# First products of a transformer layer: the statistics of x moved from VectorE to ScalarE, modulation columns by transposes, the first weights in four parts

## The chip, the cores and the metric

The kernel runs on one core of a Trainium2 chip. The metric is the device time of one execution in microseconds (us). The engines are named as the profile does: PE (TensorE, matrix products), PEld (its weight loads), DVE (VectorE), ACT (ScalarE), POOL (GpSimd) and SP (SyncE, which here issues nearly all DMA transfers). Each engine works through its own queue in order; semaphores hold it back where it needs another engine's result.

## What is computed

One layer on 256 tokens of 2048 features in float32: a gated feed-forward part (5632 hidden features), a token mixer (8 attention heads and 4 recurrent heads), and a second feed-forward part. Before each part the tokens are normalised and modulated by a shift and a scale that come from a condition vector c; after each part comes a layer norm with residual.

```python
def _modulate(x, shift, scale):
    return _layernorm(x) * (1 + scale) + shift

def _swiglu(h, w_in, w_out):
    gate, up = jnp.split(h @ w_in, 2, axis=-1)
    return (jax.nn.silu(gate) * up) @ w_out

    ada = (jax.nn.silu(c) @ w_ada + b_ada)[:, None, :]
    sh1, sc1, g1, sh2, sc2, g2, sh3, sc3, g3 = jnp.split(ada, N_ADA, axis=-1)
    h = _swiglu(_modulate(x, sh1, sc1), ffn1_w_in, ffn1_w_out)
    x = _layernorm(ALPHA * x + 0.5 * (1 + g1) * h, ln1_g, ln1_b)
    ...
```

For this document only the start matters: sh1 and sc1 (each a product of silu(c) with 2048 x 2048 of w_ada), the mean and variance of each token of x, and the first products with ffn1_w_in.

## The kernel before

The 256 tokens are two halves of 128 (a = 0, 1), one token per partition, in the tile res. Every product is made of three (mm3, L391 to L393): each operand is split into hi, a rounded copy made on ACT, and lo, the remainder made on DVE; hi by hi, hi by lo and lo by hi are added up in PSUM. PE does only these products, transposes and small sums.

The first modulation is made in four blocks j of 512 features. For a block, first_ada (L702) fetches 16 rows of w_ada, 512 KB each, one DMA transfer each (L714, L720). Row k holds 128 inputs for 512 columns of the shift and 512 of the scale. DVE adds up raw x silu(c) over the rows into acc (ada_acc, L156 on; L158 for row 0, L160 for the others; for block 0 acc lies in the tile gate). The last row is added in two halves of the columns. What remains is a sum over the 128 partitions, and the result has to stand with features on partitions: column (L754) makes it with two products per group of 128 features, acc as the stationary operand and a column of ones as the moving one (L757), and DVE adds the bias columns (L759) into scsh. In the other blocks columns (L738, L741) does so for four groups at once.

ada_acc ends in tc.keep_in_program_order(ins): the instruction is queued behind the last one that was written for the same engine before it. Other instructions are placed by a scheduler, from its own estimate of when operands are there. Where tc.manual_schedule names an engine, that engine takes its instructions in the order of writing.

Beside this, x is normalised. Eight bn_stats on DVE (L845), four for each half of the tokens, and bn_aggr (L281) give mean and variance; row_std (L280) adds EPS on DVE (L283) and takes the inverse root on POOL (L271); L848 makes -mean x root on DVE. These instructions are written before the sixteen rows. modulate_both (L307) then normalises 512 features on ACT (L311), transposes them on PE (L317), and per group of 128 features applies scale and shift (L322, ACT), makes hi (L325, ACT) and lo (L327, DVE).

The weights of the first part come as tiles of 512 inputs by 512 outputs, 1 MB, by one DMA transfer (load_w, L374), and are split two groups of 128 inputs at a time (1024 columns of free size; L145 on ACT, L146 on DVE). The first tile's weights are split inside the last step of first_ada(0), where ws_halves is advanced between the column groups; this step stands under manual_schedule for DVE and ACT (L854). first_in (L792) makes the 48 products of a tile for two PSUM tiles, and ACT copies them out (L812). There are twelve tiles in each of the four blocks.

The buffers: three of 8 KB per partition named raw, shared by the modulation rows (two rows each) and the raw weights; three named araw, which take every third pair of rows; six each of hi and lo. A transfer into a buffer is issued when the last reader of its former content is done, and SP issues in its order. PSUM has five tiles for products (mm_tile) and three for the rest (aux_tile).

## Time and profile before

| | |
|---|---|
| Time, median of 3 runs | 1940.28 us (1939.87 to 1940.95) |
| The profiled execution's own time | 1938.98 us |
| Its span in the profile | 1937.3 us |
| First product (L391) starts | 38.59 us |
| First row of w_ada added (L158) | 13.79 us |
| Last row added (L160) starts | 33.52 us |
| PE busy from 0 to 25 us | 2.46 us |
| PE busy from 25 to 50 us | 14.91 us |
| PE busy from 50 to 75 us | 25.00 us |

Times inside the profile count from the start of its span. A row of the timeline gives start, length, engine, line, operation, the tile written, the tiles read, their shapes, and in brackets how long the engine stood idle before it and what ended the wait. "x4" means that four such instructions were merged into one row. A row of a group gives busy time and, behind the comma, the mean length of one instruction in ns. "SPq" rows are issues of DMA transfers. The profiled execution was 1.3 us shorter than the median.

### The profile page before, as it was taken

To read this page: it belongs to the slowest core of one execution; us is meant where nothing else is said; L and a number is where in the kernel's file an instruction comes from. 1 tells how busy PE (TensorE), PEld (TensorE's weight loads), DVE (VectorE), ACT (ScalarE), POOL (GpSimd) and SP (SyncE) were. 2 spreads that over 40 slices of the span, in tenths; PEclk is the share of its full clock that TensorE was granted. 3 is DMA by queue.
4 is the path that set the end of the run, shared out by engine and by line. 5 is a ranking of instruction groups with operands and counts; after the bars stand their busy time and mean duration, and the time that the engine had idled before them with its cause. 6 is when DMAs were issued, how large, how long until landed. Compare 5 with 4: busy or idle time off the path is not lost.

```text
span 1937.3 us, 32182 instructions
## 1 busy us (share of the span) xinstructions
PE 1886.1 (97%) x13133; PEld 1730.2 (89%) x13133; DVE 1465.4 (76%) x1771; ACT 931.0 (48%) x1296; POOL 19.4 (1%) x37
## 2 busy tenths in 40 slices
PE   3999999999999999999999999999999999999997
PEld 3999999999988888698999776999999999988886
DVE  7778979777778899688787787867776654555776
ACT  2544354444354554745664644555444444444562
POOL 0000000000000000000000000000000000000000
PEclk9999999999999999999999999999999999999999
DMA  8998969999898898489878784997777655655552
GB/s 323 351 314 308 324 217 309 314 315 334 273 341 302 275 310 270 153 297 317 280 240 280 282 289 157 331 305 272 234 264 260 229 195 192 228 194 193 196 193 90
DMA packets 301963, 510.89 MB, mean 264 GB/s; under 512 B 10834, under 2 KB 158962, under 8 KB 300792
## 3 DMA queue, kind: packets, MB, share of 16 engines
q1 hardware_dynamic: 300952, 505.70, 77.0%
q0 software_dynamic: 864, 3.15, 0.6%
q8 instruction: 103, 1.69, 0.4%
q14 instruction: 44, 0.36, 0.1%
HBM read 506.71 MB, written 2.10 MB: 263 GB/s over the span
## 4 chain that ended last, share of the span: by engine, by line
PE 84%; DVE 8%; DMA 4%; ACT 2%; issue 1%; POOL 0%; DVEq 0%; SPq 0%; ACTq 0%; POOLq 0%
PE gu_f L393 8%; PE gu_f L392 8%; PE gu_f L391 8%; PE o_f L391 8%; PE o_f L393 8%; PE o_f L392 8%; DMA raw_s<-in_ffn_w_in_dram 3%; PE s L393 3%; PE s L391 3%; PE s L392 2%; PE pr_f L393 2%; PE pr_f L392 2%; PE pr_f L391 2%; DVE gate L160 2%; PE fh L392 2%; PE fh L393 2%
## 5 line engine op out<-in xcount | busy, mean ns | idle before, releaser
L160 DVE SCALAR_TENSOR_TENSOR acc<-ar,csil,acc 128x1024 f32<-128x1024 f32 x242 | 307.2, 1270 | 25.4 <-DMA ar<-in_w_ada_dram 24.6
L391 PE MATMUL s<-xhi_f,hi_s 128*128 128x256 f32 x768 | 214.0, 279 | 1.2 <-ACT hi_s L145 1.2
L393 PE MATMUL s<-xhi_f,lo_s 128*128 128x256 f32 x768 | 213.4, 279 | 1.6 <-DVE lo_s L146 1.5
L392 PE MATMUL s<-xlo_f,hi_s 128*128 128x256 f32 x768 | 213.3, 278 | 0.0
L393 PE MATMUL gu_f<-xhi_f,lo_f2i 128*128 128x256 f32 x768 | 212.0, 276 | 0.0
L392 PE MATMUL gu_f<-xlo_f,hi_f2i 128*128 128x256 f32 x768 | 212.0, 276 | 0.0
L391 PE MATMUL gu_f<-xhi_f,hi_f2i 128*128 128x256 f32 x768 | 212.0, 276 | 0.0
L146 DVE TENSOR_TENSOR lo_f2i<-raw_f2i,hi_f2i 128x1024 fp32r<-128x1024 f32 x96 | 117.5, 1225 | 99.0 <-ACT hi_f2i L145 98.9
L391 PE MATMUL gu_f<-xhi_f,hi_f1i 128*128 128x256 f32 x640 | 176.8, 276 | 0.0
L393 PE MATMUL gu_f<-xhi_f,lo_f1i 128*128 128x256 f32 x640 | 176.7, 276 | 0.0
L392 PE MATMUL gu_f<-xlo_f,hi_f1i 128*128 128x256 f32 x640 | 176.7, 276 | 0.0
L145 ACT CAST hi_f2i<-raw_f2i 128x1024 fp32r<-128x1024 f32 x96 | 100.8, 1050 | 137.5 <-PE gu_f L392 125.5
L145 ACT CAST hi_s<-raw_s 128x1024 fp32r<-128x1024 f32 x96 | 97.2, 1049 | 105.8 <-DMA raw_s<-in_ffn_w_in_dram 78.9
L393 PEld LDWEIGHTS s<-xhi_f,lo_s 128*128 128x128 f32 x768 | 145.1, 189 | 2.4 <-DVE lo_s L146 2.4
L391 PEld LDWEIGHTS s<-xhi_f,hi_s 128*128 128x128 f32 x768 | 145.4, 190 | 1.6 <-ACT hi_s L145 1.5
L392 PEld LDWEIGHTS s<-xlo_f,hi_s 128*128 128x128 f32 x768 | 145.6, 190 | 0.0
L392 PEld LDWEIGHTS gu_f<-xlo_f,hi_f2i 128*128 128x128 f32 x768 | 144.2, 188 | 0.1
L391 PEld LDWEIGHTS gu_f<-xhi_f,hi_f2i 128*128 128x128 f32 x768 | 144.2, 188 | 0.1
L393 PEld LDWEIGHTS gu_f<-xhi_f,lo_f2i 128*128 128x128 f32 x768 | 144.2, 188 | 0.0
L146 DVE TENSOR_TENSOR lo_s<-raw_s,hi_s 128x1024 fp32r<-128x1024 f32 x96 | 114.5, 1221 | 36.5 <-ACT hi_s L145 34.2
L145 ACT CAST hi_f1i<-raw_f1i 128x1024 fp32r<-128x1024 f32 x80 | 83.3, 1050 | 116.6 <-PE gu_f L392 66.7
L146 DVE TENSOR_TENSOR lo_f2o<-raw_f2o,hi_f2o 128x1024 fp32r<-128x1024 f32 x86 | 105.3, 1224 | 43.2 <-ACT hi_f2o L145 43.1
(483 smaller groups left out, 5336.6 us busy)
## 6 DMA issues: line engine op xcount, KB each, us to landing
ar<-in_w_ada_dram SPq DMA_DIRECT2D x288, 512.0 KB, 5.9
raw_s<-in_ffn_w_in_dram SPq DMA_DIRECT2D x48, 1024.0 KB, 5.4
raw_f2i<-in_ffn_w_in_dram SPq DMA_DIRECT2D x48, 1024.0 KB, 5.1
raw_f1o<-in_ffn_w_out_dram SPq DMA_DIRECT2D x44, 1024.0 KB, 8.0
raw_f2o<-in_ffn_w_out_dram SPq DMA_DIRECT2D x44, 1024.0 KB, 5.1
raw_f1i<-in_ffn_w_in_dram SPq DMA_DIRECT2D x40, 1024.0 KB, 7.8
raw_mxo<-in_w_out_dram SPq DMA_DIRECT2D x16, 1024.0 KB, 7.9
raw_fh<-in_ffn_w_in_dram SPq DMA_DIRECT2D x16, 1024.0 KB, 7.8
```

Of the source, the lines that this page charges most:

```text
L145: S.copy(hi, src)
L146: V.tensor_tensor(out=lo, in0=src, in1=hi.bitcast(F32), op=ALU.subtract)
L160: ins = V.scalar_tensor_tensor(out=acc, in0=raw, scalar=csil[:, k:k + 1], in1=acc, op0=ALU.mult, op1=ALU.add)
L391: PE.matmul(o, ah, bh, start=start, stop=False)
L392: PE.matmul(o, ah, bl, start=False, stop=False)
L393: return PE.matmul(o, al, bh, start=False, stop=stop)
```

## The change

The statistics of x are made on ScalarE: an Identity pass that adds up, two small multiplications (mean and minus mean), a Square pass with minus the mean as bias that adds up, and a multiplication to the variance, for each half of the tokens. row_std runs without bn_aggr, one half after the other. The output of the two passes goes to a part of hT that is not in use yet.

The columns of block 0 are made by transposes: two per group of 128 features into a PSUM tile of its own (one aux_tile, three mm_tile), a sum along the free dimension on DVE, and the bias added by DVE.

The first weights come by four transfers of 256 KB, and are split one group of 128 inputs at a time; the transfers and the first rounded copy are written ahead of the first group's scale and shift, the others between the groups.

```diff
     def row_std(mv, rs, st, tag):
-        V.bn_aggr(mv, st)
-        yield
+        if st is not None:
+            V.bn_aggr(mv, st)
+            yield
...
-        cps = aux_tile(f"cp{j}"), mm_tile(f"cq{j}") if j == 0 else None
+        cps = [aux_tile(f"cp{j}")]
...
+        cps += [mm_tile(f"cq{q}") for q in range(3)]
+
         def column(q):
-            cp = cps[q % 2][:, q:q + 2]
             for v in range(2):
-                PE.matmul(cp[:, v:v + 1], acc[:, v, q * P:(q + 1) * P], ones[:, 0:1], start=True, stop=True)
-            k = 4 * j + q
-            V.tensor_tensor(out=scsh[:, 0:2, k:k + 1], in0=cp.unsqueeze(2), in1=bcol[:, 0:2, k:k + 1], op=ALU.add)
+                PE.transpose(cps[q][:, v * P:(v + 1) * P], acc[:, v, q * P:(q + 1) * P], ident)
+            cs = scsh[:, 0:2, q:q + 1]
+            V.tensor_reduce(out=cs, in_=cps[q][:, :2 * P].rearrange("p (v n) -> p v n", v=2), axis=AX.X, op=ALU.add)
+            V.tensor_tensor(out=cs, in0=cs, in1=bcol[:, 0:2, q:q + 1], op=ALU.add)
 
         column(0)
-        next(mb)
-        column(1)
-        next(mb)
-        next(mb)
-        column(2)
-        next(ws, None)
-        next(mb)
-        column(3)
-        next(mb)
-        next(ws, None)
-        for _ in mb:
-            pass
+        next(ws)
+        for q in range(4):
+            next(mb)
+            if q < 3:
+                column(q + 1)
+            next(mb)
+            next(ws)
+            next(ws, None)
         yield
...
-    def ws_halves():
-        it = first_w(0, 0)
-        for _ in range(2):
-            ws.extend(next(it) for _ in range(2))
+    def first_ws():
+        raw = wp.tile([P, 4, 512], F32, tag="raw", bufs=3, name="raw_first")
+        for k in range(4):
+            SP.dma_start(raw[:, k, :], W1[k * P:(k + 1) * P, :512])
+        parts = [[wp.tile([P, 2, 512], F32R, tag=t, bufs=6, name=f"{t}_first{h}") for h in range(2)]
+                 for t in ("hi", "lo")]
+        for k in range(4):
+            hi, lo = (p[k // 2][:, k % 2, :] for p in parts)
+            S.copy(hi, raw[:, k, :])
             yield
-
-    fa = first_ada(0, ws_halves())
+            V.tensor_tensor(out=lo, in0=raw[:, k, :], in1=hi.bitcast(F32), op=ALU.subtract)
+            ws.append((k, hi, lo))
+            yield
+
+    fa = first_ada(0, first_ws())
...
-    sts = [stat_tile(f"x{a}") for a in range(2)]
+    sq = hT[:, 0:8, :].rearrange("p f t -> p (f t)")
     for a in range(2):
-        for q in range(4):
-            V.bn_stats(sts[a][:, q, :], res[:, a, q * 512:(q + 1) * 512])
-    together(*[row_std(mvx[a], rs0[a][:, 0:1], sts[a], f"x{a}") for a in range(2)])
+        xs = small(10, "sums", f"sums_x{a}")
+        S.activation(sq, res[:, a, :], AF.Identity, accum_out=xs[:, 0:1])
+        S.mul(mvx[a][:, 0:1], xs[:, 0:1], 1.0 / D)
+        S.mul(xs[:, 1:2], xs[:, 0:1], -1.0 / D)
+        S.activation(sq, res[:, a, :], AF.Square, bias=xs[:, 1:2], accum_out=xs[:, 2:3])
+        S.mul(mvx[a][:, 1:2], xs[:, 2:3], 1.0 / D)
+    for a in range(2):
+        for _ in row_std(mvx[a], rs0[a][:, 0:1], None, f"x{a}"):
+            pass
     for a in range(2):
         V.scalar_tensor_tensor(out=rs0[a][:, 1:2], in0=mvx[a][:, 0:1], scalar=-1.0, in1=rs0[a][:, 0:1],
                                op0=ALU.mult, op1=ALU.mult)
```

## The prediction

> **What bounds the kernel now.** First the page, by engine and by its chain that ended last:
>
> ```profile
> PE 1886.1 (97%) x13133; PEld 1730.2 (89%) x13133; DVE 1465.4 (76%) x1771; ACT 931.0 (48%) x1296; POOL 19.4 (1%) x37
> ...
> PE 84%; DVE 8%; DMA 4%; ACT 2%; issue 1%; POOL 0%; DVEq 0%; SPq 0%; ACTq 0%; POOLq 0%
> ```
>
> PE is busy for 97% of the span, so whatever the change can win or lose lies in the small rest, most of it before the first product. That stretch is read from the chain in order of time (start, length, what):
>
> ```profile
> 6.24 2.47 DVE st_x L845 x4
> ...
> 13.79 0.76 DVE gate L158
> ...
> 33.52 0.76 DVE gate L160
> ...
> 34.41 1.00 PE cp L757 x4
> ...
> 37.60 0.95 ACT hi_s L145
> ...
> 38.59 0.58 PE s L391
> ...
> 44.97 0.21 PE s L393
> ...
> 45.47 0.12 PE s L393
> ```
>
> The reader is to see one thread: x lands, its statistics (DVE and POOL), the sixteen rows of the first modulation block on DVE (13.79 to 34.9), their columns, the normalised x, the first weights, the first product at 38.59. Products then step at 0.21 us, and from 45.1 on at 0.12.
>
> How the rows hang on the statistics is in the timeline:
>
> ```profile
> 10.08 2.46 DVE L845 BATCH_NORM_STATS2 st_x<-res 128x6 f32<-128x512 f32 x4
> 12.58 0.26 DVE L281 BATCH_NORM_AGGREGATE mv_x<-st_x 128x2 f32<-128x24 f32 x1
> 12.88 0.15 DVE L283 TENSOR_SCALAR mv_x<-mv_x 128x1 f32<-128x1 f32 x1
> ...
> 13.70 0.16 DVE L848 SCALAR_TENSOR_TENSOR mr_x<-mv_x,mr_x 128x1 f32<-128x1 f32 x1 [0.67 <-POOL mr_x L271]
> ...
> 14.58 6.57 DVE L160 SCALAR_TENSOR_TENSOR gate<-ar,csil,gate 128x1024 f32<-128x1024 f32 x5
> ```
>
> Row 0 (L158, 13.79) starts 0.09 us after L848 for the second half of x. That is no accident: ada_acc ties each row behind the VectorE instruction written before it, and the last one written before row 0 is that L848. DVE takes its queue in order, so **row 0 waits for the statistics of both halves of x**, whoever computes them. From there the rows run without a gap, one per 1.31 us (five in 6.57).
>
> **The change, part by part.**
>
> *1. Statistics on ScalarE.* Eight bn_stats and two aggregations leave DVE (2.47 us and 0.26 us for each half). L283 and L848 stay on DVE, POOL keeps its pow, and row 0 stays tied behind L848. So the freed DVE time is not used by the rows: DVE now waits for ACT. The new ACT work is not in the trace at its size; its nearest rows:
>
> ```profile
> L819 ACT ACTIVATE hT<-hT 128x512 f32<-128x512 f32 x12 | 7.3, 631 | 2.0 <-DVE hT L814 2.0
> L545 ACT ACTIVATE sq<-res,sums 128x768 f32<-128x768 f32 x8 | 7.5, 939 | 1.0 <-DVE res L541 0.8 <-DVE sums L551 0.2
> L545 ACT ACTIVATE sq<-res,sums 128x512 f32<-128x512 f32 x4 | 2.9, 725 | 25.3 <-DVE sums L544 25.3
> L545 ACT ACTIVATION_READ_ACCUMULATOR sq<-res,sums 128x1 f32 x12 | 2.2, 186 | 0.0
> L1241 ACT ACTIVATE table<-ident 128x1 f32<-128x1 f32 x1 | 0.2, 203 | 0.0
> ```
>
> From 512 to 768 elements ACT takes 939 - 725 = 214 ns more, 0.836 ns an element. An Identity over 2048 without a bias column is 631 + 1536 x 0.836 = 1.92 us; a Square with one is 939 + 1280 x 0.836 = 2.01 us. Each is followed by a read of the accumulator (0.19), and there are three multiplications of one column (0.20 each). End to end that is 1.92 + 2.01 + 0.37 + 0.61 = 4.9 us for half of x. ACT instructions overlap by about 0.1 us at a joint:
>
> ```profile
> 775.32 0.73 ACT L545 ACTIVATE sq<-res,sums 128x512 f32<-128x512 f32 x1 [12.48 <-DVE sums L544]
> 775.95 0.19 ACT L545 ACTIVATION_READ_ACCUMULATOR sq<-res,sums 128x1 f32 x1
> ```
>
> (775.32 + 0.73 is 0.10 past 775.95). With all six joints overlapped it is 4.3 us. Most joints are between an instruction and the reader of its result, so I take 4.6, and keep 4.3 to 4.9. The first half starts when x lands (6.24), the second right behind it, since its data are there by 10.08: done at 6.24 + 9.2 = 15.4. L283 follows at 15.5 against 12.88, and the rest of the thread (POOL, L848, row 0) is unchanged at 0.91 us. **Row 0 starts at 16.4 instead of 13.79: +2.6 us (+2.0 to +3.2).** The rows then take the 20.5 us from 13.79 to 34.28 again, so the first half of the last row, call its end e, moves from 34.28 to 36.9.
>
> Weighing a rule against this: the Trainium skill, page "ScalarE: Activation LUTs", section "Rules for kernel authors", sends plain additions and multiplications to VectorE. The trace agrees: 2.7 us on DVE against 4.6 on ACT for the same half of x.
>
> What hides the rows' transfers:
>
> ```profile
> ar<-in_w_ada_dram SPq DMA_DIRECT2D x288, 512.0 KB, 5.9
> ```
>
> Rows 8 and 9 go out when rows 0 and 1 are used (18.5 to 19.1), land 5.9 later at 25, and are needed at 16.4 + 8 x 1.31 + 0.6 (bias columns) = 27.5. Rows 14 and 15 go out at 27.5, land at 33.5, are needed at 35.3. They cost nothing; if a transfer took 2 us more it would show. On SP's queue the bias rows' transfer waits for a DVE cast that stands behind bn_stats now; without them it and rows 6 and 7 go out sooner, which changes nothing while DVE waits for ACT. POOL gets nothing new.
>
> *2. Columns by transposes, weights in quarters.*
>
> ```profile
> 18.12 1.91 PE L317 MATMUL tp<-ident,xf 128*128 128x128 f32 x8
> ...
> 33.52 1.41 DVE L160 SCALAR_TENSOR_TENSOR gate<-ar,csil,gate 128x512 f32<-128x512 f32 x2
> 35.44 0.16 DVE L759 TENSOR_TENSOR scsh<-cp,bcol 128x2 f32<-128x2 f32 x1 [0.50 <-PE cp L757]
> ...
> 41.57 0.75 DVE L327 TENSOR_TENSOR xlo_f<-xf,xhi_f 128x256 fp32r<-128x256 f32 x2
> ...
> 47.39 0.28 PE L393 MATMUL s<-xhi_f,lo_s 128*128 128x256 f32 x1
> ...
> L196 DVE TENSOR_REDUCE scsh<-at 128x4 f32<-128x512 f32 x16 | 10.7, 684 | 2.8 <-PE at L193 2.8
> L1069 DVE TENSOR_REDUCE nm<-s 128x1 f32<-128x256 f32 x8 | 3.2, 406 | 0.0
> L146 DVE TENSOR_TENSOR lo_gu<-raw_gu,hi_gu 128x512 fp32r<-128x512 f32 x20 | 12.9, 687 | 6.5 <-ACT hi_gu L145 6.5
> ```
>
> Per column group PE has two transposes of 0.24 instead of four passes in 1.00 us; DVE gains a sum over 256 elements out of PSUM: between half of L196's 684 ns and the whole of it, taken as 0.42 us, near L1069, which has the same 256 elements from SBUF in 406 ns. The four groups put 1.7 us more on DVE and take 4 x (1.00 - 0.48) = 2.1 off PE. For group 0 the transposes end at e + 0.64, under the last row's second half on DVE (to e + 0.66); sum and addition end at e + 1.3 (now 35.60, e + 1.3): the same. Then xf 0.6 and xhi 0.4. Now two such groups and a cast of 1024 weights (0.95) stand before the first product (38.59 is e + 4.3); afterwards the first quarter of the weights is cast ahead of it, so **the first product comes at e + 2.4 instead of e + 4.3: -1.9 us**. The weights allow it: their buffer is free after row 9 (30.1), four issues and 5.9 us bring them by 37.1, their cast is due at e + 1.3 = 38.2. The three more issues on SP stand ahead of the next block's rows, which wait for the buffer of rows 12 and 13 (35.3) anyway. The three more PSUM tiles and the first tile's two are the pool's five; the next two are wanted only at the second tile.
>
> So the first product falls at 39.3 against 38.59, +0.7. Behind it DVE has per quarter a sum and addition (0.55), xlo (0.35 to 0.4) and a split of 512 weights (0.62 to 0.69): the last one ends at e + 7.7 = 44.6, against xlo at 42.3 now. PE has 48 products in its first tile and needs 10.1 us for them at 0.21, so it is fed. First tile ended: +0.7 (48.2 against 47.5).
>
> *3. What is late next.* The buffers of the raw weights come free later, and with them the next transfers:
>
> ```profile
> 40.00:42.00 2.00, 2.00 (x10) 2.00 (x10) 1.78 (x5) 1.26 (x3) 0.00 (x0) 1.00 0.00 0
> ...
> 41.68 0.88 SPq L720 DMA_DIRECT2D ar<-in_w_ada_dram  x2
> ...
> 44.33 0.37 SPq L374 DMA_DIRECT2D raw_s<-in_ffn_w_in_dram  x1
> ...
> 47.23 0.37 SPq L374 DMA_DIRECT2D raw_s<-in_ffn_w_in_dram  x1
> ...
> 56.38 2.00 ACT L145 CAST hi_s<-raw_s 128x1024 fp32r<-128x1024 f32 x2 [2.50 <-DMA raw_s<-in_ffn_w_in_dram]
> 58.52 1.08 ACT L812 COPY hT<-s 128x512 f32<-128x512 f32 x2
> ```
>
> DMA stands still at 40 to 42 (0 GB/s, last column): it waits for buffers, not the reverse. The three free at 41.68, 44.33 and 47.23 become free at 44.6 (+2.9), 46.6 (+2.3: two rows behind it) and 49.0 (+1.8: ACT is done earlier in its queue). So the fourth tile's weights, now here at 56.38 and cast at 57.4, come 1.8 to 2.9 later. PE leaves the third tile at 58.5, so they have 1.1 us to spare: PE is pushed to +0.7 to +1.8. **Sum: +2.6 - 1.9 = +0.7 by PE's own order, +0.7 to +1.8 by its supply; I take +1.4.**
>
> Later nothing takes that back:
>
> ```profile
> 103.07 1.69 PE cp L741 x16
> ...
> 230.25 1.24 DVE lo_s L146
> ```
>
> From 103 to 231 the chain goes by DMA and DVE, but it starts from PE's own columns at 103, so it moves as a whole with PE; after that it is PE. The profiled execution took 1938.98 us (span 1937.3 and 1.7 around it): 1940.4 for it. It lies 1.3 under the median of 1940.28, so against that the forecast is **1941.7 us**. A measurement of this kernel tells about 0.2% (3.9 us) from no change: I forecast no difference that can be told.
>
> **Rivals.**
>
> - *The wait is hidden.* ACT's joints all overlap (row 0 at +2.0) and the spare 1.1 us covers the supply: 2.0 - 1.9 = +0.1, so 1940.4 us. For it: the short joints of L545. Against: the results are read at once.
> - *PE stays slow longer.* The step of 0.21 lasts until 45.1 now, after 5 us without a gap, while the granted clock reads 1.00 (40 to 42, above). If the products come in quarters with gaps of 0.2 us, all 48 run at 0.21: first tile ended at e + 13.7 = 50.6, +3.1, so 1943.4 us. Against: the second half of the tile can fill the gaps. The Trainium skill, "TensorE: Matmul & The Clock Gate", section "What's actually happening", has the clock rise only after a busy window of about 3.4 us that runs freely, and its "Part 4: PE-mode transpose" does not count transposes as busy. The two steps agree; that the transposes count for nothing no run here shows.
> - *Slower beyond doubt: ACT's statistics are a longer thread.* If every reader on ACT waits for the result before it, a half of x takes 6.0 us, not 4.6: row 0 at +5.4, first product +3.5, supply 4.6 to 5.7 less 1.1 spare: +4.2, so 1944.5 us. It decides from about 5.9 us per half. For it: L848 waits 0.67 for a pow of 0.56. Against: 0.1 us overlap at L545.
>
> ```profile
> 30.00:32.00 2.00, 0.00 (x0) 0.00 (x0) 1.96 (x2) 0.00 (x0) 0.00 (x0) 1.00 1.05 389
> ```
>
> - *Faster: the rows do not wait.* If row 0 starts as it lands, DMA sets the rows: 10.6 MB (x, the bias rows, 16 x 0.52) at the 389 GB/s of this stretch (last column), counted from 2.2, end at 29.4, with the first half of its last row done by 31.2; e moves by -3 and the first product by -5, of which later supply returns 1: 1936.3 us. Then the change would do what its words suggest. Against it stands the tie in ada_acc.
>
> **Chances.** Forecast 0.45, hidden wait 0.25, slow PE 0.14, long statistics 0.10, rows free 0.04, another order of the later instructions 0.02. The last two cases beside the long statistics are left out of the range in part: 1939.2 (the hidden wait, less the spread of the runs) to 1945.0 (the long statistics). Faster by over 0.2%: the free rows and half of the reordering, 0.05. Slower: the long statistics and the worst of the slow PE, 0.14. Within: 0.81.
>
> **What would show it.** In the new timeline: DVE idle until L283 at about 15.5, row 0 at 16.4, two ACT passes of 1.9 to 2.0 us for each half of x, the last row's first half ended at 36.9, the first product 2.4 us later, a wait for transfers near 58. Row 0 before 13.8 would make the whole forecast wrong; a pass much above 2.0 us would make its size wrong.

## The result, and the profile after

The changed kernel takes 1945.74 us (median of 8 runs, 1942.42 to 1948.82), the kernel before 1940.07 us (median of 8 on the same chip, 1935.58 to 1942.35). The ratio is 1.0034, with an interval of 1.0023 to 1.0045: slower, by more than the 0.2% that the prediction took as the least that can be told, and 0.7 us above the top of the range. The ratios and intervals here are worked out from all runs, so a ratio can differ from the quotient of the two medians (1.0029 here). The forecast had been 1941.7 us and no difference.

The profiled execution took 1942.81 us (span 1941.1), against 1938.98 (span 1937.3) before. Its page, busy time by engine and the chain that ended last:

```profile
PE 1885.0 (97%) x13125; PEld 1727.3 (89%) x13125; DVE 1461.8 (75%) x1767; ACT 941.6 (49%) x1313; POOL 19.4 (1%) x37
...
PE 85%; DVE 7%; DMA 4%; ACT 2%; issue 1%; POOL 0%; SPq 0%; DVEq 0%; ACTq 0%; POOLq 0%
```

Nothing in these shares tells where the time went. The timeline does (start, length, engine, line, what; in brackets the idle time before it and its releaser). The lines of the changed kernel stand some 10 below those of before: L158 and L160 are still the rows, L861 is the old L848, L392 to L394 are the products.

```profile
6.28 1.91 ACT L852 ACTIVATE hT<-res 128x2048 f32<-128x2048 f32 x1 [4.19 <-DMA res<-in_x_dram]
...
8.29 1.28 ACT L108 ACT_TABLE_LOAD   x1
9.59 0.18 ACT L108 ACTIVATE csil<-cps 128x16 f32<-128x16 f32 x1
...
9.99 2.00 ACT L855 ACTIVATE hT<-res,sums_x 128x2048 f32<-128x2048 f32 x1
...
14.11 0.80 ACT L312 ACTIVATE xf<-res,mr_x 128x512 f32<-128x512 f32 x1
...
17.49 0.15 DVE L284 TENSOR_SCALAR mv_x<-mv_x 128x1 f32<-128x1 f32 x1 [4.09 <-ACT mv_x L856]
...
18.31 0.16 DVE L861 SCALAR_TENSOR_TENSOR mr_x<-mv_x,mr_x 128x1 f32<-128x1 f32 x1 [0.67 <-POOL mr_x L271]
18.39 0.75 DVE L158 TENSOR_SCALAR gate<-ar,csil 128x1024 f32<-128x1024 f32 x1
...
38.68 0.66 PE L759 MATMUL cp<-ident,gate 128*128 128x128 f32 x2 [17.54 <-DVE gate L160]
...
41.15 0.80 PE L392 MATMUL s<-xhi_f,hi_first 128*128 128x256 f32 x2 [0.54 <-ACT xhi_f L326]
...
54.89 1.07 ACT L811 COPY hT<-s 128x512 f32<-128x512 f32 x2 [4.36 <-PE s L394]
55.85 2.00 ACT L145 CAST hi_s<-raw_s 128x1024 fp32r<-128x1024 f32 x2
...
56.96 0.39 PE L392 MATMUL s<-xhi_f,hi_s 128*128 128x256 f32 x1 [0.89 <-ACT hi_s L145]
...
58.22 0.50 PE L394 MATMUL s<-xhi_f,lo_s 128*128 128x256 f32 x2 [0.52 <-DVE lo_s L146]
```

The reader is to see the thread of the forecast, each step later than forecast. The two passes over x take 1.91 and 2.00 us, as worked out. But the Silu of c (L108) stands behind the first pass and has a table load of its own (1.28 us), and the normalisation of the first half (L312) stands inside the second half's statistics. Row 0 starts right behind L861, at 18.39. The first product comes at 41.15, and PE stands still twice in the third tile, 0.89 and 0.52 us; before it had no such wait. PE's waits from 42 to 250 us (total, times, longest), of the changed kernel and then of the kernel before:

```profile
PE s L394 <- DVE lo_s L146: 2.0, 4, 0.8
PE s L392 <- ACT hi_s L145: 1.5, 2, 0.9
PE s L392 <- DVE hT L813: 1.4, 2, 1.2
```

```profile
PE s L393 <- DVE lo_s L146: 1.5, 2, 0.8
PE s L391 <- ACT hi_s L145: 0.6, 1, 0.6
```

To follow one delay through the kernel, the table has five places: row 0, the first product, and the start of the column products (L741 before, L742 after) of blocks 1, 2 and 3, which PE reaches after one, two and three blocks. It has a row for each kernel below too; the last column is the ratio to the kernel before, timed on the same chip.

| kernel | row 0 | first product | block 1 | block 2 | block 3 | ratio (interval) |
|---|---|---|---|---|---|---|
| before | 13.79 | 38.59 | 102.91 | 172.39 | 242.33 | 1 |
| after | 18.39 | 41.15 | 106.86 | 176.87 | 248.17 | 1.0034 (1.0023 to 1.0045) |
| e1_act_order | 16.40 | 40.29 | 107.74 | 180.79 | 252.74 | 1.0028 (1.0016 to 1.0041) |
| e2_rows_free | 10.17 | 35.27 | 101.32 | 172.52 | 247.21 | 0.9999 (0.9990 to 1.0008) |
| e3_columns_only | 13.65 | 36.76 | 102.42 | 175.48 | 247.94 | 1.0001 (0.9988 to 1.0013) |
| e4_statistics_only | 18.36 | 42.77 | 106.03 | 179.24 | 250.30 | 1.0016 (1.0008 to 1.0025) |
| f1_after_old_order | 18.23 | 40.98 | 109.22 | 183.17 | 254.32 | 1.0027 (1.0018 to 1.0035) |
| f2_rows_free_old_order | 10.05 | 35.15 | 101.63 | 171.31 | 243.98 | 1.0003 (0.9994 to 1.0012) |
| f3_before_new_order | 13.73 | 38.53 | 103.92 | 173.64 | 244.12 | 1.0013 (1.0004 to 1.0023) |
| f4_columns_old_order | 13.66 | 36.77 | 103.34 | 172.28 | 245.00 | 0.9998 (0.9987 to 1.0009) |
| g1_before_half_rows | 13.73 | 38.53 | 102.63 | 170.88 | 238.90 | 0.9965 (0.9953 to 0.9977) |
| g2_after_half_rows | 18.22 | 40.98 | 106.50 | 175.05 | 243.05 | 1.0000 (0.9990 to 1.0011) |
| g3_free_half_rows | 10.11 | 35.21 | 100.85 | 169.64 | 237.64 | 0.9966 (0.9953 to 0.9979) |
| h4_before_own_place | 13.78 | 38.58 | 102.61 | 172.69 | 243.06 | 1.0000 (0.9991 to 1.0008) |
| h1_after_own_place | 18.34 | 41.11 | 105.54 | 173.66 | 246.18 | 1.0017 (1.0007 to 1.0027) |
| h2_columns_own_place | 13.70 | 36.82 | 101.56 | 171.20 | 244.11 | 1.0001 (0.9991 to 1.0011) |
| h3_free_own_place | 10.27 | 35.38 | 100.06 | 168.51 | 243.54 | 0.9986 (0.9977 to 0.9994) |
| j0_before_half_again | 13.60 | 38.40 | 102.36 | 171.28 | 239.28 | 0.9960 (0.9947 to 0.9972) |
| j1_after_own_half | 18.24 | 41.01 | 105.64 | 173.94 | 243.79 | 0.9987 (0.9978 to 0.9995) |
| j2_free_own_half | 10.37 | 35.46 | 99.75 | 168.48 | 238.58 | 0.9951 (0.9940 to 0.9963) |

Read along the second row against the first: +4.60 at row 0, +2.56 at the first product, +3.95 at block 1 (the 1.41 us of the third tile), +4.48 at block 2, +5.84 at block 3. At the end of the profiled execution it is +3.8: behind block 3 the kernel before waited 3.0 us at two places of the mixer (L1077, L1228), the changed one 1.1. The medians are 5.7 apart. The places in the table are of one execution each; executions of the same kernel lie some us apart (the kernel before from 1934.7 to 1945.2), so differences of 1 us at blocks 2 and 3 of a single row mean little. The profiled execution of f1 was its longest, 1949.91 against a median of 1943.84.

### The profile page after: what moved, and what is told of

It reads as the page before. It is cut to its first block, busy times and chain, and to the rows that moved or that the text cites. A ratio compares the mean times of both kernels' runs of the same rounds, so it can differ in the third digit from the quotient of the medians.

```text
span 1941.1 us, 32179 instructions
## 1 busy us (share of the span) xinstructions
PE 1885.0 (97%) x13125; PEld 1727.3 (89%) x13125; DVE 1461.8 (75%) x1767; ACT 941.6 (49%) x1313; POOL 19.4 (1%) x37
## 3 DMA queue, kind: packets, MB, share of 16 engines
q8 instruction: 103, 1.69, 0.4%
## 4 chain that ended last, share of the span: by engine, by line
PE 85%; DVE 7%; DMA 4%; ACT 2%; issue 1%; POOL 0%; SPq 0%; DVEq 0%; ACTq 0%; POOLq 0%
PE gu_f L394 8%; PE gu_f L393 8%; PE gu_f L392 8%; PE o_f L392 8%; PE o_f L394 8%; PE o_f L393 8%; DMA raw_s<-in_ffn_w_in_dram 2%; PE s L394 2%; PE s L392 2%; PE s L393 2%; PE pr_f L394 2%; PE pr_f L393 2%; PE pr_f L392 2%; PE fh L393 2%; PE fh L394 1%; PE fh L392 1%
## 5 line engine op out<-in xcount | busy, mean ns | idle before, releaser
L160 DVE SCALAR_TENSOR_TENSOR acc<-ar,csil,acc 128x1024 f32<-128x1024 f32 x242 | 307.2, 1270 | 24.3 <-DMA ar<-in_w_ada_dram 23.6
L394 PE MATMUL gu_f<-xhi_f,lo_f2i 128*128 128x256 f32 x768 | 212.0, 276 | 0.0
L392 PE MATMUL gu_f<-xhi_f,hi_f2i 128*128 128x256 f32 x768 | 212.0, 276 | 0.0
L392 PE MATMUL s<-xhi_f,hi_s 128*128 128x256 f32 x752 | 208.6, 277 | 3.0 <-ACT hi_s L145 1.5
L394 PE MATMUL s<-xhi_f,lo_s 128*128 128x256 f32 x752 | 208.0, 277 | 2.0 <-DVE lo_s L146 2.0
L393 PE MATMUL s<-xlo_f,hi_s 128*128 128x256 f32 x752 | 207.6, 276 | 0.0
L392 PE MATMUL gu_f<-xhi_f,hi_f1i 128*128 128x256 f32 x640 | 176.8, 276 | 0.0
L394 PE MATMUL gu_f<-xhi_f,lo_f1i 128*128 128x256 f32 x640 | 176.7, 276 | 0.0
L392 PEld LDWEIGHTS s<-xhi_f,hi_s 128*128 128x128 f32 x752 | 141.2, 188 | 3.8 <-ACT hi_s L145 2.0
L392 PEld LDWEIGHTS gu_f<-xhi_f,hi_f2i 128*128 128x128 f32 x768 | 144.2, 188 | 0.1
L394 PEld LDWEIGHTS gu_f<-xhi_f,lo_f2i 128*128 128x128 f32 x768 | 144.2, 188 | 0.0
L394 PEld LDWEIGHTS s<-xhi_f,lo_s 128*128 128x128 f32 x752 | 141.1, 188 | 2.8 <-DVE lo_s L146 2.8
L393 PEld LDWEIGHTS s<-xlo_f,hi_s 128*128 128x128 f32 x752 | 141.2, 188 | 0.0
```

Source lines behind the costliest of these rows:

```text
L160: ins = V.scalar_tensor_tensor(out=acc, in0=raw, scalar=csil[:, k:k + 1], in1=acc, op0=ALU.mult, op1=ALU.add)
L392: PE.matmul(o, ah, bh, start=start, stop=False)
L393: PE.matmul(o, ah, bl, start=False, stop=False)
L394: return PE.matmul(o, al, bh, start=False, stop=stop)
```

## The experiments

### One part at a time

**e1_act_order**: the changed kernel, with the Silu of c held ahead of the statistics and the normalisation behind them.

```diff
-        S.activation(sq, res[:, a, :], AF.Identity, accum_out=xs[:, 0:1])
+        tc.keep_in_program_order(S.activation(sq, res[:, a, :], AF.Identity, accum_out=xs[:, 0:1]))
...
-            S.activation(n[:, a, :], res[:, a, j * 512:(j + 1) * 512], AF.Identity, bias=rs[a][:, 1:2],
-                         scale=rs[a][:, 0:1])
+            ins = S.activation(n[:, a, :], res[:, a, j * 512:(j + 1) * 512], AF.Identity, bias=rs[a][:, 1:2],
+                               scale=rs[a][:, 0:1])
+            if v == j == 0:
+                tc.keep_in_program_order(ins)
```

> The changed kernel with ScalarE's order pinned: Silu of c ahead of the statistics, the normalising of block 0 behind them. Theory (the loss is the thread of the start: ScalarE's order added a second table load of 1.28 us and a pass of 0.71 us ahead of row 0): row 0 of w_ada at 16.3 us instead of 18.4, one table load less, first product at 39.1 instead of 41.15, and the time 2 us below the changed kernel, about +2 to +4 us against before. Rival (the loss is made in the blocks behind, by another order of transfers and splits, whatever the start does): row 0 at 16.3 as well, but the time stays at +5 to +6 us.

Measured: 1946.99 us, ratio 1.0028; row 0 at 16.40, first product at 40.29. The order on ACT is worth the 2.0 us at row 0 (18.39 to 16.40) that the forecast lacked. A little over half of it is lost again before the first product, because DVE now comes to the copy of the bias columns before these are there. e1, its timeline:

```profile
18.15 0.31 DVE L122 COPY bcol<-bps 128x144 f32<-128x144 f32 x1 [1.00 <-PE bps L121]
```

And the time does not follow: at block 1 the kernel is not earlier than the changed one. What is put right at row 0 does not decide the time by itself, at least not with the order of later instructions that came with it.

**e2_rows_free**: e1, with row_std and L861 written behind the third and the fourth step of the rows, so that no row waits for the statistics.

```diff
-    for a in range(2):
-        for _ in row_std(mvx[a], rs0[a][:, 0:1], None, f"x{a}"):
-            pass
...
     for i in range(8):
         next(fa)
         if i == 2:
             load_bcol()
+            for a in range(2):
+                for _ in row_std(mvx[a], rs0[a][:, 0:1], None, f"x{a}"):
+                    pass
+        if i == 3:
+            for a in range(2):
+                V.scalar_tensor_tensor(out=rs0[a][:, 1:2], in0=mvx[a][:, 0:1], scalar=-1.0, in1=rs0[a][:, 0:1],
+                                       op0=ALU.mult, op1=ALU.mult)
```

> As e1, and in addition the last steps of the statistics on VectorE are written behind row 5 instead of ahead of row 0, so that no row waits for them. Theory (row 0 waits for nothing but the tie): row 0 at 10 to 10.5 us when its transfer lands, rows then at the transfers' rate of 1.35 us, the last row's first half ended at 31 to 32, first product at 33.5 to 34.5 instead of 38.6 before; time 3 to 4.5 us below before. Rival (the transfers and splits of the later tiles absorb what the start wins): first product as above, but PE waits that much more between 45 and 250 us, and the time is within 1 us of before.

Measured: 1939.91 us, ratio 0.9999; row 0 at 10.17, first product at 35.27, 3.3 us earlier than before. Nothing of these 3.3 us is left at the end: +0.1 at block 2, +4.9 at block 3.

**e3_columns_only**: the changed kernel with the statistics as before, on DVE.

```diff
-    sq = hT[:, 0:8, :].rearrange("p f t -> p (f t)")
+    sts = [stat_tile(f"x{a}") for a in range(2)]
     for a in range(2):
-        xs = small(10, "sums", f"sums_x{a}")
-        S.activation(sq, res[:, a, :], AF.Identity, accum_out=xs[:, 0:1])
...
+        for q in range(4):
+            V.bn_stats(sts[a][:, q, :], res[:, a, q * 512:(q + 1) * 512])
+    together(*[row_std(mvx[a], rs0[a][:, 0:1], sts[a], f"x{a}") for a in range(2)])
```

> The change without its first part: statistics on VectorE as before, columns by transposes and first weights in quarters. Theory (this part is worth 1.9 to 2.0 us at the first product): row 0 at 13.8, last row's first half ended at 34.3, first product at 36.6 instead of 38.6, time 1 to 2 us below before. Rival (the columns' longer VectorE work and the later weights give it back at the third tile): first product as above, time at or above before.

**e4_statistics_only**: the changed kernel with columns and first weights as before.

```diff
             for v in range(2):
-                PE.transpose(cps[q][:, v * P:(v + 1) * P], acc[:, v, q * P:(q + 1) * P], ident)
...
+                PE.matmul(cp[:, v:v + 1], acc[:, v, q * P:(q + 1) * P], ones[:, 0:1], start=True, stop=True)
...
-    def first_ws():
...
+    def ws_halves():
+        it = first_w(0, 0)
+        for _ in range(2):
+            ws.extend(next(it) for _ in range(2))
```

> The change's first part alone: statistics on ScalarE, columns and weights as before. Theory: row 0 at 18.4 as in the changed kernel if ScalarE keeps that order, first product 4.6 us later than before at 43.2, time 4.5 to 7 us above before. Rival (the start does not matter to the end): time within 1 us of before.

Measured: e3 1940.90 us, ratio 1.0001; e4 1942.85 us, ratio 1.0016. The columns and weights bring the first product from 38.59 to 36.76, as forecast (-1.8 against -1.9), and the kernel is not faster. The statistics bring it to 42.77 (+4.2), and the kernel is 0.16% slower, some 3 us. Every kernel with the columns-and-weights part reaches block 1 1.3 to 3.1 us later, counted from its first product, than the kernel before (64.32 us; e4 63.26): after 65.71, e1 67.45, e2 66.05, e3 65.66. So **this part gives most of its gain back inside the first block** (e3 1.3 of 1.8 us). That was the question for the rest.

### Is it the order of the later instructions?

With another start the scheduler also places later splits, rows, copies and transfers otherwise. In the changed kernel ACT copies the second tile out (54.89) ahead of the casts of the third (55.85). In the next four kernels the later instructions of DVE, ACT, SP and PE are pinned in a given order.

```diff
+def later_order(tc, start):
+    seq = {}
+    for i in list(tc.nc.cur_bb.bb.instructions)[start:]:
...
+                if prev is not None:
+                    tc.add_manual_dep(seq[e][k], prev.name,
+                                      mybir.DependencyInfo(mybir.DependencyClass.NoSync, mybir.DependencyReason.DATA),
+                                      reason="later_order")
+                prev = seq[e][k]
...
     with tc.manual_schedule(engines={mybir.EngineType.DVE, mybir.EngineType.Activation}):
         next(fa)
+    start = len(tc.nc.cur_bb.bb.instructions)
...
     lnp.release()
+    later_order(tc, start)
```

> The changed kernel whole, with one addition: behind the start (the last step of first_ada for block 0) DVE, ACT, SP and PE take their instructions in the order in which the kernel before takes them, to the middle of block 3 at least. Theory ORDER (the changed start makes the scheduler place later splits, copies, rows and transfers otherwise, and that costs what the first product's delay does not explain): the two waits of 0.89 and 0.52 us in the third tile go, and only the first product's delay is left: +2.6 us on the kernel before, 1942.4, ratio 1.0013. Theory TRANSFERS (up to 250 us the transfers set the pace; while the rows wait for the statistics their buffers stay full, and by 30 us the changed kernel has moved 9.05 MB where the kernel before has moved 10.51; 1.46 MB at some 320 GB/s are 4.6 us that are never caught up): the order is of no use, 1945 to 1946, ratio 1.0025 to 1.0032, and the columns of block 3 come at 247 us or later as in the changed kernel (248.2) against 242.3.

> The kernel in which the rows do not wait for the statistics (first product at 35.3 us, time as before, 1939.9), with the later instructions of DVE, ACT, SP and PE in the order of the kernel before. ORDER: the gain of the first product comes through, -3.3 us: 1936.6, ratio 0.9983, and no waits of 0.89 and 0.52 in the third tile. TRANSFERS: its transfers are only 0.07 MB ahead of the kernel before at 30 us and 0.5 MB at 40, so at most 0.2 to 1.6 us are to be had: 1938.2 to 1939.6, and PE waits elsewhere for what it gained, above all at 150 to 165 and at 230 us.

> The kernel before whole, start and all, with the later instructions of DVE, ACT, SP and PE in the order of the changed kernel. ORDER: 3 us longer than the kernel before, 1943, ratio 1.0015, with waits of 0.9 and 0.5 us in the third tile. TRANSFERS: nothing but the third tile's waits, which the transfers' lag swallows later: 1940 to 1941, ratio 1.0000 to 1.0007.

> Columns by transposes and the first weights in four parts alone, statistics on DVE as before (first product at 36.8, -1.8; time 1940.9 with the scheduler's own order), with the later instructions in the order of the kernel before. ORDER: the -1.8 us come through: 1938.0, ratio 0.9991, no waits of 0.89 and 0.52 us in the third tile. TRANSFERS: the transfers stood level with those of the kernel before (14.06 against 13.73 MB at 40 us), so at most 1 us: 1939 to 1940, with longer waits near 160 and 232 us than before (0.76 and 1.36).

Measured: f1 1943.84 us (1.0027), f2 1938.44 (1.0003), f3 1941.59 (1.0013), f4 1938.85 (0.9998), against 1939.20. The changed kernel's order in the kernel before costs 2.4 us (f3), about what ORDER expected, and makes the very waits of 0.89 and 0.52 us in the third tile. But taking it out of the others gains nothing that can be told from no change, against ORDER, and a wait in the third tile stays. The kernel before, then f3, then f1:

```profile
49.66 2.00 ACT L145 CAST hi_s<-raw_s 128x1024 fp32r<-128x1024 f32 x2 [1.22 <-DMA raw_s<-in_ffn_w_in_dram]
```

```profile
51.95 1.07 ACT L864 COPY hT<-s 128x512 f32<-128x512 f32 x2 [4.36 <-PE s L445]
52.91 3.90 ACT L197 CAST hi_s<-raw_s 128x1024 fp32r<-128x1024 f32 x4
...
54.02 0.39 PE L443 MATMUL s<-xhi_f,hi_s 128*128 128x256 f32 x1 [0.89 <-ACT hi_s L197]
```

```profile
46.32 0.88 SPq L772 DMA_DIRECT2D ar<-in_w_ada_dram  x2
48.27 0.37 SPq L426 DMA_DIRECT2D raw_s<-in_ffn_w_in_dram  x1
...
55.83 2.00 ACT L196 CAST hi_s<-raw_s 128x1024 fp32r<-128x1024 f32 x2 [5.29 <-DMA raw_s<-in_ffn_w_in_dram]
...
56.92 0.38 PE L443 MATMUL s<-xhi_f,hi_s 128*128 128x256 f32 x1 [1.72 <-ACT hi_s L196]
```

In f1 ACT is free, waits 5.29 us for the third tile's weights, and casts them when they land, at the very time (55.83 against 55.85) at which the changed kernel cast them behind its copies. So the changed kernel has two causes for its wait, and each is enough alone: the order on ACT, as in f3, and that **the third tile's weights come late**. They left at 48.27 and took 7.5 us; before, they left at 44.33 and were cast at 49.66, 5.3 us later. In front of them go two rows of the next block, and both wait for raw buffers. The rows wait for the one that holds the first tile's weights until their last split; the third tile's weights wait for the one with the first two rows of the next block, which DVE adds right behind that split, from 46.17 to 48.23.

### Is it the transfers?

Added up from the GB/s of ten-us windows, the changed kernel had moved 9.05 MB by 30 us, the kernel before 10.51: the rows' buffers stay full while the rows wait for the statistics. The windows (DMA share and GB/s last), of the kernel before and of the changed one:

```profile
10.00:30.00 20.00, 2.21 (x10) 1.81 (x10) 18.83 (x25) 1.63 (x2) 0.56 (x1) 1.00 1.05 383
...
100.00:170.00 70.00, 69.24 (x607) 68.84 (x606) 58.76 (x65) 30.91 (x39) 0.00 (x0) 1.00 0.94 324
```

```profile
10.00:30.00 20.00, 2.47 (x10) 1.77 (x10) 11.94 (x18) 8.18 (x12) 1.11 (x2) 1.00 0.88 311
...
100.00:170.00 70.00, 68.59 (x602) 68.18 (x602) 57.46 (x63) 30.88 (x40) 0.00 (x0) 1.00 0.93 321
```

From 100 to 170 us both kernels move 321 to 324 GB/s at a DMA share of 0.93 to 0.94; there is little left to catch up with, and by 250 us the changed kernel is still 1.8 MB behind (79.1 against 80.9). That lag alone proves nothing: at some 320 GB/s it is 5.6 us, the delay itself in other units. Three kernels leave out 24 transfers of 512 KB (of each two rows of blocks 1 to 3 the first serves for both), with the later order of the kernel before.

```diff
                 for h in range(2):
                     k = 2 * kk + h
-                    SP.dma_start(raw[:, h], src[k * P:(k + 1) * P])
-                raws = [raw[:, h] for h in range(2)]
+                    if j and h:
+                        skipped.append(len(tc.nc.cur_bb.bb.instructions))
+                    else:
+                        SP.dma_start(raw[:, h], src[k * P:(k + 1) * P])
+                raws = [raw[:, h if j == 0 else 0] for h in range(2)]
```

> The kernel before with half of the modulation transfers left out in blocks 1 to 3: of each two rows of w_ada only the first is fetched, and used for both, so the modulation of these blocks is not the reference's; all other instructions stay, in the order of the kernel before. 24 transfers of 512 KB fewer, 12.6 MB of the 82 MB up to 250 us. This is the base for the two others. TRANSFERS: PE's waits near 161 and 230 us (2.1 us in all) go: 1937 to 1938. BUFFERS (what holds PE back later is not the transfers but the loop of casts, splits and rows on ACT and DVE that frees the buffers, and this has not become shorter): 1939 to 1940, waits as before.

> The changed kernel, later instructions in the order of the kernel before, with the same 24 transfers left out (rows of blocks 1 to 3 used twice, so the modulation of these blocks is not the reference's). TRANSFERS: with transfers to spare, the lag of 1.46 MB at 30 us is made up, and only the first product's delay of 2.6 us is left against the base with the same transfers left out: base + 2.6. BUFFERS: base + 4.6, as with all transfers (1943.8 against 1939.2).

> The kernel whose rows do not wait for the statistics, later instructions in the order of the kernel before, with the same 24 transfers left out (rows of blocks 1 to 3 used twice, so the modulation of these blocks is not the reference's). TRANSFERS: the first product's gain of 3.3 us comes through against the base: base - 3.3. BUFFERS: base - 0 to 0.8, as with all transfers (1938.4 against 1939.2).

Measured: g1 1933.18 us, g2 1939.94, g3 1931.94, so +6.8 and -1.2 on the base. By their medians both theories fail: g1 gains more than PE's waits held, g2 loses more than either said. The table tells the blocks apart. From the columns of block 1 to those of block 3 the base takes 136.3 us, g2 136.6 and g3 136.8; with all transfers it was 139.4 before and 141.3 after. So with transfers to spare the changed start costs next to nothing in blocks 1 and 2: **there it is the transfers**, as TRANSFERS said, or the buffers that they go into: the rows left out also take up fewer araw buffers, and these runs do not tell the two apart. But block 0 stays 1.4 to 1.5 us longer than the base's 64.10 (65.52 and 65.64), with waits in the third tile (0.3 + 0.3, 0.8 + 0.3): **in block 0 it is something else**. Why g2's median lies 6.8 us over the base when its columns of block 3 are 4.15 later stays open; its profiled execution was one of its shortest (1936.8), that of g1 its longest (1934.8).

### The raw buffer of the first weights

If the raw buffers are what holds the third tile's weights back, the first tile's weights must not take one. Here they go to a part of hT that is first written by the fifth tile.

```diff
-        raw = wp.tile([P, 4, 512], F32, tag="raw", bufs=3, name="raw_first")
+        raw = hT[:, 8:16, :].rearrange("p (k h) t -> p k (h t)", k=4)
```

All four kernels have the later order of the kernel before; h4 is the kernel before with only this change, written for its own single transfer.

> The kernel before, with the first tile's raw weights in a part of hT that is written only from the fifth tile on, in place of one of the three raw buffers; nothing else is changed, and the order of every queue is that of the kernel before. The buffer loop is one transfer ahead at the start. BUFFERS-AT-THE-START (weights and rows of the next block leave as the raw buffers come free, and the first tile's weights hold one of the three until their last split): the standstill of the transfers at 40 to 42 us goes, the cumulative bytes at 60 us are 0.5 to 1 MB more than before (23.3 MB at 70 us), and part of PE's waits near 161 and 230 us (2.1 us) goes: 1937 to 1939. PACE (later transfers go at a pace of their own whatever the start): 1939 to 1940, waits as before.

> The changed kernel, the first tile's raw weights in the idle part of hT, later instructions in the order of the kernel before. BUFFERS-AT-THE-START: the third tile's weights, which left at 48.3 to 48.4 us, leave 2 us or more earlier, PE's waits of 1.4 to 2.0 us in the third tile go, and so do some of the later ones: 1941 to 1942 (the first product's delay of 2.6 alone), against 1943.8 with the raw buffer. PACE: 1943 to 1945.

> Columns by transposes and first weights in four parts, statistics as before on DVE, the first tile's raw weights in the idle part of hT, later instructions in the order of the kernel before. BUFFERS-AT-THE-START: no waits of 1.69 and 0.30 us in the third tile, the first product's gain of 1.8 us comes through: 1.8 us less than the kernel before with the same place for the weights, 1935.5 to 1937. PACE: 1938 to 1940, with the gained time spent in waits near 160 and 232 us.

> The kernel whose rows do not wait for the statistics, the first tile's raw weights in the idle part of hT, later instructions in the order of the kernel before. BUFFERS-AT-THE-START: no waits of 1.08 and 0.30 us in the third tile, the first product's gain of 3.3 us comes through: 3.3 us less than the kernel before with the same place for the weights, 1934 to 1936, ratio 0.997 to 0.998, faster than both kernels. PACE: 1938 to 1940, with the gained time spent in waits near 160 and 231 us.

Measured: h4 1939.16 us (1.0000), h1 1940.93 (1.0017), h2 1939.01 (1.0001), h3 1936.77 (0.9986), against 1939.38. h1, its timeline:

```profile
36.40 0.37 SPq L426 DMA_DIRECT2D raw_s<-in_ffn_w_in_dram  x1
39.17 0.88 SPq L772 DMA_DIRECT2D ar<-in_w_ada_dram  x2
48.39 0.37 SPq L426 DMA_DIRECT2D raw_s<-in_ffn_w_in_dram  x1
...
53.53 2.00 ACT L196 CAST hi_s<-raw_s 128x1024 fp32r<-128x1024 f32 x2 [2.63 <-DMA raw_s<-in_ffn_w_in_dram]
```

The expectation was wrong in one thing: the third tile's weights leave no earlier (48.39), since they still wait for the second row that DVE adds (to 48.36). But the two rows in front of them left at 39.17 instead of 46.32, so the weights do not share the DMA engines with them and land after 5.1 us instead of 7.5. PE waits nowhere in the third tile of h1, h2 and h3. From first product to block 1 it is 64.43, 64.74 and 64.68 us, where f1, f4 and f2 had 68.24, 66.57 and 66.48. BUFFERS-AT-THE-START holds for block 0, and **h3 is faster than both kernels**: 2.6 us less than before, 0.14% with an interval of 0.06% to 0.23%. h1 loses 1.6 us by the medians and 3.3 by its ratio, about its first product's delay of 2.5 (f1: 4.6 and 5.2), though the intervals of f1 and h1 overlap. h2 and h3 stayed short of the 1.8 and 3.3 us expected. For h4 it was wrong: the kernel before had no wait there to lose. And of h2's and h3's lead of 1.2 and 3.9 us at block 2 nothing is left at block 3 (+1.8 and +1.2), where PE waits again. So the trace of h3 does not show where the 2.6 us of its median come from; behind block 3 it takes 1692.2 us against 1695.0 before, the longest such stretch of all these traces. h3 there, the timeline, and the windows with the granted clock (column behind PE's count):

```profile
228.88 0.58 PE L445 MATMUL s<-xhi_f,hi_s 128*128 128x256 f32 x1 [2.77 <-ACT hi_s L196]
...
230.13 0.58 PE L447 MATMUL s<-xhi_f,lo_s 128*128 128x256 f32 x1 [0.46 <-DVE lo_s L197]
```

```profile
228.00:230.00 2.00, 0.80 (x2) 0.72 1.01 385
230.00:232.00 2.00, 1.87 (x8) 0.50 0.58 224
232.00:234.00 2.00, 2.00 (x11) 0.50 0.81 257
234.00:236.00 2.00, 2.00 (x12) 0.57 0.89 304
236.00:238.00 2.00, 2.00 (x20) 1.00 0.97 339
```

A wait of 2.77 us costs more than itself: the granted clock falls to 0.50, and PE does 8 to 12 products in 2 us instead of 20 until 236.

### Both taken away

> The base of the next two, on their chip: the kernel before with 24 transfers of w_ada rows left out in blocks 1 to 3 (of each two rows the first is used twice, so the modulation of these blocks is not the reference's). As measured: ratio 0.9965 on the kernel before, some 1933 us, columns of block 3 at 238.9 us, no waits of PE from 42 to 330 us.

> The changed kernel with both suspected limits taken away: first tile's raw weights in the idle part of hT, and the 24 transfers left out (rows of blocks 1 to 3 used twice, modulation of these blocks not the reference's); later order of the kernel before. BOTH LIMITS (the raw buffer at the start, then the transfers): nothing is left but the first product's delay of 2.5 us: columns of block 3 at 241.4 (base + 2.5) and base + 2.5 in time, against base + 4.2 at the columns with the raw buffer. ANOTHER CAUSE: base + 4 or more at the columns of block 3.

> The kernel whose rows do not wait for the statistics, with both suspected limits taken away in the same way (rows of blocks 1 to 3 used twice, modulation of these blocks not the reference's). BOTH LIMITS: the first product's gain of 3.3 us comes through whole: columns of block 3 at 235.6 (base - 3.3), and base - 3.3 in time; with the raw buffer it was base - 1.3 at the columns. ANOTHER CAUSE: base - 1.5 or less of a gain at the columns of block 3.

Measured: j0 1932.85 us, j1 1937.31, j2 1930.56: +4.5 and -2.3 on the base, where both limits alone asked for +2.5 and -3.3. At block 2 they hold: +2.66 and -2.80, with +2.61 and -2.94 at the first product, so the start's shift comes through two blocks whole. In block 2 both lose 1.9 and 2.1 us on the base (69.85 and 70.10 against 68.00). In both, PE's longer steps between products in block 2 add up to that loss: 1.9 us in j1 and 2.2 in j2, against 0.2 in j0, g1 and g2. The trace shows where they come from; j0, then j2:

```profile
167.66 0.37 SPq L430 DMA_DIRECT2D raw_s<-in_ffn_w_in_dram  x1
172.48 1.05 ACT L201 CAST hi_s<-raw_s 128x1024 fp32r<-128x1024 f32 x1 [3.64 <-DVE hT L878]
...
225.23 2.00 ACT L201 CAST hi_s<-raw_s 128x1024 fp32r<-128x1024 f32 x2 [8.58 <-DVE hT L878]
```

```profile
164.54 0.37 SPq L433 DMA_DIRECT2D raw_s<-in_ffn_w_in_dram  x1
172.38 1.05 ACT L201 CAST hi_s<-raw_s 128x1024 fp32r<-128x1024 f32 x1 [6.69 <-DMA raw_s<-in_ffn_w_in_dram]
...
225.43 1.99 ACT L201 CAST hi_s<-raw_s 128x1024 fp32r<-128x1024 f32 x2 [8.84 <-DMA raw_s<-in_ffn_w_in_dram]
```

One transfer of weights at the start of block 2 takes 7.7 us to land in j2 and 7.9 in j1; in j0 it takes 4.8 at most, in g2 and g3 5.2 and 5.0. With that the 2.8 us by which j2 led are gone: from there its rows and weights leave when those of j0 do (182.62 against 182.72, 220.26 against 220.28), and PE, which comes earlier, waits, 0.76 us for the weights cast at 225.43. At 198 it waits 0.35 us for DVE, which has no pause from 190 to 200:

```profile
190.00:195.00 5.00, 4.98 (x44) 4.78 (x43) 5.00 (x7) 0.27 (x1) 0.00 (x0) 1.00 0.59 227
195.00:200.00 5.00, 4.65 (x41) 4.45 (x40) 5.00 (x6) 1.74 (x2) 0.00 (x0) 1.00 0.84 288
```

So another cause is left in block 2, as ANOTHER CAUSE had it, of about 2 us: again weights that land late. g2 and g3, in which that transfer took 5 us, took 68.00 for the block. Why it is slow in j1 and j2, with half of the rows left out, stays open.

## Why the prediction was wrong, step by step

Two steps failed: the work on ACT ahead of row 0, and the supply behind the first product.

**Row 0 (+2.6; it was +4.6): the first failed step.** "the second right behind it, since its data are there by 10.08: done at 6.24 + 9.2 = 15.4" took ACT to hold nothing but the statistics. The sizes were right: passes of 1.92 and 2.01 against 1.91 and 2.00 measured, and in e1, where ACT does nothing else before, row 0 starts at 16.40, as forecast. What was missed stands in the rows at 8.29 and 14.11: a table load of 1.28 us and 0.71 us of normalisation. Silu stood first on ACT before; the scheduler put a pass that needs another function ahead of it. The Trainium skill, page "ScalarE: Activation LUTs", section "What ACT_TABLE_LOAD costs", gives 1283 ns for a load, as here, and 1380 ns of draining on top for a switch; no drain shows here, the Silu starts at 9.59, 0.02 us after the load. Every other instruction that is ready for the engine should have been listed, since the change opens gaps for them.

**First product, e + 2.4.** Nearly right: 38.54 (end of the last row's first half) to 41.15 is 2.6 us, and e3 alone gave -1.8 for -1.9. With the 2.0 us of row 0, the first product came at +2.56 instead of +0.7.

**The buffers.** Their times were right, shifted by the same 1.9: 46.49, 48.43 and some 50.7 for the forecast 44.6, 46.6 and 49.0. Wrong was which weights were tested against them. The forecast gave the fourth tile's weights 1.1 us to spare and did not look at the third tile's, which go into the second of these buffers. Before, their first cast was done at 50.7 and PE there at 52.9, 2.2 us to spare. In f1 they come 6.2 us later (55.83 against 49.66: 3.9 by the buffer, 2.2 because rows leave just ahead of them), and PE only 2.3: a wait of 1.7 by this sum, 1.72 in the trace. In the changed kernel it is 1.41 where 0.7 was taken. The waits near 58 that the forecast named did come, at 56.96 and 58.22, but for the third tile's weights, not the fourth's. It also explains most of what the columns part loses in block 0: in e3 and f4 the first product comes 1.8 us earlier, the third tile's weights leave only 0.3 us earlier (44.04 and 44.05 against 44.33), because DVE, whose rows free their buffer, has more to do before. That is not all: h2, without that wait, is no faster than the kernel before either.

**"Later nothing takes that back": the second failed step.** The forecast put what comes behind block 1 at nothing. It adds 1.9 us (3.95 at block 1, 5.84 at block 3). The quoted standstill of DMA at 40 to 42 was read as transfers that have time. They have it there, but not in general: 383 GB/s at 10 to 30 us, 324 from 100 to 170, and the kernel before is close to its transfers at 160 and 230 us (waits of 2.1 us). In g1, with fewer transfers, these waits are gone.

**The rivals.** *The wait is hidden* fails at row 0 (+4.6, not +2.0). *Rows free* does not hold in the changed kernel; where the experiments made the rows free (e2) the first product came 3.3 us earlier, not 5, and the time did not follow. That h3 reached 1936.77, near its 1936.3, is luck. *Slower beyond doubt* had the size (1944.5) by luck, with another mechanism: the readers on ACT do not wait longer, there was other work between. *PE slow longer* did not occur in the profiled execution: the steps of 0.21 ended at 46.8, 5.7 us after the first product, 6.5 before.

So of the 5.84 us at block 3, where 1.4 were forecast, 2.56 are the first product (2.0 of row 0's delay come from the order on ACT, and e1 shows that taking them away alone gains nothing), 1.41 the third tile's late cast, and 1.9 came later. The third tile's part is shown by f3 and the h kernels. The last part is shown less well: in the g kernels fewer transfers take it away, in the j kernels some 2 us come back in block 2, and all of it is read from single executions.

## What to carry to other kernels

A delay at the start is not only a shift: while a chain of sums waits, its buffers stay full and transfers stand still, and where later transfers run near their pace it may not be made up; so work out the bytes moved by a given time, not only the first product. When an engine's queue gets new work that waits, list everything that is ready for it, because the scheduler may put it between, table loads too. When a first product is brought forward, find the last reader of the buffer for which the second and third tiles' weights wait, and what else leaves just ahead of them: unless these are earlier too, the gain can end there.

## What the runs showed of the hardware

A PE wait that is long enough costs its length again. f1, the windows around its wait in the third tile (1.72 and 0.30 us; PE, PEld, DVE, ACT, POOL, granted clock, DMA share, GB/s):

```profile
56.00:58.00 2.00, 0.96 (x6) 0.72 (x6) 1.10 (x1) 2.00 (x3) 0.00 (x0) 1.00 1.03 377
58.00:60.00 2.00, 1.82 (x9) 1.82 (x10) 2.00 (x3) 0.79 (x2) 0.00 (x0) 0.62 1.05 402
60.00:62.00 2.00, 2.00 (x12) 2.00 (x11) 1.74 (x2) 0.00 (x0) 0.00 (x0) 0.53 1.05 387
62.00:64.00 2.00, 2.00 (x19) 2.00 (x19) 0.48 (x1) 1.56 (x2) 0.00 (x0) 1.00 1.04 386
```

Twenty products go into 2 us at full clock; from 58 to 64 come 9, 12 and 19. f4 had the same waits (1.69 and 0.30 us) and kept its clock; over the 12 us around them f1 loses 1.6 us more, to the clock alone, on top of 2.0 us of waiting. Waits of 0.89 and 0.52 us (after and e3, third tile) did not lower it. Between 42 and 300 us of the twenty traces the smallest pair of waits behind which it fell was 1.12 and 0.75 us (f1, at 170), the largest behind which it did not 1.70 and 0.76 (f4, at 233). So the point from which it falls lies near 2 us of waiting here, and is met in some executions and not in others. The Trainium skill, "TensorE: Matmul & The Clock Gate", section "What's actually happening", has the clock halve after an idle window of about 3.4 us that runs freely. The halving and the chance in it agree; but 2.0 us of waiting in two pieces was enough here.

The scatter between executions goes with the clock too, though that it comes from such waits is not shown. Of the 35 runs of the kernel before on the chip of the f kernels, those with a mean granted clock of 0.998 (17), 0.997 (14) and 0.996 (3) took 1938.5, 1939.8 and 1942.0 us on average. All 21 runs of g1, g3, j0 and j2, which fetch less, had 0.998.

And a transfer's flight can depend on what left just before it: the same 1 MB took 7.5 us behind two rows issued 2 us earlier (f1) and 5.1 us behind two rows issued 9 us earlier (h1). That is not the whole of it: the transfer of block 2 above took 5.0 us in g3 and 7.7 in j2, both times behind one row issued 2.6 and 2.3 us earlier.
